# A float32 encoder trunk: the feed-forward input product turned round, with the input normalised before it is transposed

## The chip, the core and the metric

The kernel runs on one core of a Trainium2 chip. The metric is device time in microseconds (us) of one execution, from profiled and unprofiled runs of the same program; lower is better. TensorE is the matrix engine (PE in the profile, its weight loads PEld), VectorE is DVE, ScalarE is ACT, GpSimd is POOL, and SP is the engine that issues most DMA transfers.

## What is computed

256 tokens of width 1024 pass through four layers. Each layer has a feed-forward block, a token mixer (HGRN2, differential attention, pooling, then HGRN2 again) and a second feed-forward block: twelve sub-layers, eight of them feed-forward. Every sub-layer is normalised before and after, all in float32.

```python
def rmsnorm(x, w):
    y = xf * lax.rsqrt(jnp.mean(xf * xf, axis=-1, keepdims=True) + NORM_EPS)
    return (y * w)

def swiglu(x, w_in, w_out):          # w_in 1024 x 5632, w_out 2816 x 1024
    g, u = jnp.split(x @ w_in, 2, axis=-1)
    return (jax.nn.silu(g) * u) @ w_out

h = h + 0.5 * rmsnorm(swiglu(rmsnorm(h, gn[0]), ffn1_w_in[i], ffn1_w_out[i]), gn[1])
h = h + rmsnorm(mixer(rmsnorm(h, gn[2])), gn[3])
h = h + 0.5 * rmsnorm(swiglu(rmsnorm(h, gn[4]), ffn2_w_in[i], ffn2_w_out[i]), gn[5])
```

## The kernel before

**A float32 product in three.** Every float32 operand of a large product is kept as two float32r parts, high and low (`wh`, `wl` for weights, `xTh`, `xTl` for the transposed input, a pair of `hT` tiles for the hidden values). A product is the sum of three float32r products: high by high, high by low, low by high (`passes`, L203).

**Tiles.** The tokens lie in two tiles of 128. The residual stream is `h[0]`, `h[1]` (128 tokens x 1024). `pre` (L265) transposes the raw `h` of a token tile, eight 128x128 blocks on PE (L238), and splits the result into `xTh`, `xTl` (L274, L275). The norm before a sub-layer is not applied there: its gain is multiplied into the weights when these are split (L174 on ACT, L175 on DVE, each in pieces of 128x512), and its factor per token, 1/rms, is applied to the product at its end (`factors`, L278; `self.rs[t]` in `glu`).

**Weights.** All weights are used once per run and stream from DRAM in units of 1 MB (`fetch`, L148, issued by SP). `pump` splits a unit into two pairs `wh`, `wl`: units that carry a gain by L174 and L175, the others in pieces of 128x1024 by L169 on ACT and L170 on DVE.

**The feed-forward block** (`ffn`, L371) goes through eleven chunks of 256 hidden columns. For chunk c and token tile t there are these steps:

- `p` (`project`, L210, products on L207): the normalised input times 512 columns (256 of the gate half, 256 of the other half). The stationary operand is a 128x128 block of `xT`, the moving one 512 columns of weights; eight blocks of the inner dimension times three gives 24 products into one PSUM bank `s1` (shown as `s`), with tokens on the partitions. `glu` (L361) makes sigmoid (ACT, L366) and two multiplications (DVE, L367, L368) of it: `hh`, 128 tokens x 256.
- `t` (`split_T`, L241): two transposes of `hh` on PE (L238), then the split into the parts `hT` on ACT and DVE (L247, L248).
- `s` (`emit_out`, L219, products on L231): `hT` as the stationary operand times 1024 columns of the second weights into `acc[t]`, 12 products.

The steps are written out by hand in a string; from chunk 2 on, one chunk is

```python
todo += f" p{c}0 p{c}1 t{c}0"
todo += f" s{c - 1}0 s{c - 1}1 t{c}1" if c < e - 1 else f" t{c}1"
```

The last chunk (e = 10) is done by token tile, so that the residual of tile 0 runs beside the products of tile 1.

**Between sub-layers.** `residual` (L284) squares `acc` in two halves (ACT, L293), multiplies by the gain (DVE, L294, tile `tt`), makes the factor on POOL in three operations (L259, L261, L262) and adds into `h` in four pieces (DVE, L299). `turn` then calls `pre` for that token tile behind the next block of products. So the transposes of tile 0 stand behind the last input product of tile 1, and those of tile 1 behind the first block of the next sub-layer. This happens at eleven boundaries, twice each.

**Who sets the order.** The program is written as a list of operations; a scheduler places each on its engine's queue by priority and by its own estimate of when operands are there, and each engine then works through its queue in order. Code under `high_priority` is placed early; the splitting of weights is placed late (by LAG).

Of the kernel before, what the change touches and what calls it, by code (L numbers as in the profile page):

```python
# [9 lines left out]
F32 = mybir.dt.float32  # L10
# [30 lines left out]
# columns of the constant array  # L41
# [43 lines left out]
def grouped(w, cols):  # L85
    """[.., 1024, n] -> [.., chunk, half, 128, 4 k-tiles, 512]; cols lists each chunk's column runs."""
# [28 lines left out]
class Trunk:  # L115
    def __init__(self, ctx, tc, a, out, plan):
# [16 lines left out]
        self.units, self.loaded, self.ready, self.live, self.place = [], [], [], {"in": 0, "out": 0}, None  # L133
# [3 lines left out]
    def room(self, kind):  # L137
        """an FFN's second weights live in that FFN's own pool; kind is "in" or that FFN's place"""
# [4 lines left out]
    def fetch(self, parts=1):  # L143
        src, kind, gain = self.units.pop(0)
# [4 lines left out]
        self.loaded.append((r, kind, gain))  # L149

    def pump(self):
        nc = self.nc
        while True:
# [4 lines left out]
            if self.loaded and self.room(self.loaded[0][1]):  # L158
                r, kind, gain = self.loaded.pop(0)
# [4 lines left out]
                for j in range(2):  # L164
# [3 lines left out]
                    if gain is None:  # L168
                        nc.scalar.copy(wh, x)  # L169
                        nc.vector.tensor_sub(wl, x, wh.bitcast(F32))  # L170
                    else:
                        for k in range(2):
                            s, g = slice(k * 512, k * 512 + 512), self.gains[:, gain + 2 * j + k:gain + 2 * j + k + 1]
                            nc.scalar.activation(wh[:, s], x[:, s], AF.Copy, scale=g)  # L174
                            nc.vector.scalar_tensor_tensor(wl[:, s], x[:, s], g, wh[:, s].bitcast(F32),  # L175
                                                           op0=ALU.mult, op1=ALU.subtract)
# [20 lines left out]
    def in_units(self, w, i, j, n):  # L197
        """n chunks of an input product, gained by norm_gains[i, j]"""
        g = (i * 3 + j // 2) * KD
# [685 lines left out]
```

## Time and profile before

| | |
|---|---|
| device time, median of 3 runs | 2004.21 us (2003.1 to 2005.03) |
| the profiled execution, first to last instruction (span) | 2004.7 us |
| PE busy | 1977.9 us, 99% of the span |
| weight loads on PE (beside the products) | 1630.4 us, 81% |
| DVE busy | 1325.6 us, 66% |
| ACT busy | 1177.7 us, 59% |
| POOL busy | 81.7 us, 4% |
| granted PE clock, mean | 0.999 |
| moved by DMA | 358.56 MB, 179 GB/s |

The profiled execution is 0.5 us above the median of the runs. The page lists busy time by engine, the clock in 40 slices, the chain of work that ended last, and the costliest groups of instructions by line. A group's mean duration on PE is that of one product alone; products overlap, so the distance from one product's start to the next one's is what a stream of them costs.

### The profile page before, as it was taken

The page shows a single profiled execution, that of the slowest core. Times are in us where ns is not written, and L with a number is a line of the kernel's source. Part 1 is how long each engine was busy: PE and PEld are TensorE (multiplying, and loading weights), DVE is VectorE, ACT ScalarE, POOL GpSimd, SP SyncE. Part 2 cuts the span into 40 slices and gives each one's busy share as a digit, 9 for nine tenths or more (in the row PEclk, how much of TensorE's full clock was granted, in tenths as well). Part 3 has the DMA queues.
Part 4 walks back from the last instruction along what each step waited for, and adds up shares of the span by engine and source line. Part 5 has one row for each costly group of instructions (what it writes and reads, how often), then busy time and mean ns, then how long its engine had stood idle before and what let it go on. Part 6 is the DMA issues. An engine that isn't in the chain of part 4 may idle for free.

```text
span 2004.7 us, 25370 instructions
## 1 busy us (share of the span) xinstructions
PE 1977.9 (99%) x9320; PEld 1630.4 (81%) x9320; DVE 1325.6 (66%) x2356; ACT 1177.7 (59%) x2080; POOL 81.7 (4%) x189
## 2 busy tenths in 40 slices
PE   8999999999999999999999999999999999999998
PEld 6888888888888887788888888788888888888886
DVE  7765666866576658776667655676576657768652
ACT  7655786755565556665556545555465557767541
POOL 0000001000000000100000000000000000010000
PEclk9999999999999999999999999999999999999999
DMA  7753342755365534375536554465555534426540
GB/s 275 267 188 123 149 168 85 263 213 186 141 232 187 188 123 155 114 265 210 187 139 232 188 189 146 144 252 198 180 180 209 188 127 162 177 85 253 217 149 22
DMA packets 55003, 358.56 MB, mean 179 GB/s; under 512 B 7008, under 2 KB 10080, under 8 KB 13024
## 3 DMA queue, kind: packets, MB, share of 16 engines
q1 hardware_dynamic: 54016, 356.31, 49.4%
q8 instruction: 74, 1.21, 0.2%
q10 hardware_dynamic: 864, 0.64, 0.1%
q14 instruction: 49, 0.40, 0.1%
HBM read 355.86 MB, written 1.06 MB: 178 GB/s over the span
## 4 chain that ended last, share of the span: by engine, by line
PE 88%; issue 5%; DVE 3%; ACT 2%; POOL 1%; DMA 1%; POOLq 0%; DVEq 0%; SPq 0%; ACTq 0%
PE s L207 54%; PE acc L231 24%; PE tr L238 3%; PE acc L207 3%; DVE wl L175 1%; PE acc L633 1%; PE acc L577 1%; POOL ro L262 1%; ACT wh L174 0%; PE acc L817 0%; DMA h<-in_x_dram 0%; ACT junk L293 0%; DVE wl L170 0%; PE acc L627 0%; DMA lbraw<-in_hgrn_lb_raw_dram 0%
## 5 line engine op out<-in xcount | busy, mean ns | idle before, releaser
L207 PE MATMUL s<-wh,xTh 128*128 128x512 f32 x1792 | 712.0, 397 | 3.4 <-ACT wh L174 3.4
L207 PE MATMUL s<-wh,xTl 128*128 128x512 f32 x1792 | 701.0, 391 | 0.0
L207 PE MATMUL s<-wl,xTh 128*128 128x512 f32 x1792 | 699.9, 391 | 0.3 <-DVE wl L175 0.3
L175 DVE SCALAR_TENSOR_TENSOR wl<-raw,gains,wh 128x512 fp32r<-128x512 f32 x896 | 622.3, 745 | 66.3 <-ACT wh L174 66.0
L174 ACT ACTIVATE wh<-raw,gains 128x512 fp32r<-128x512 f32 x896 | 594.1, 720 | 92.3 <-PE s L207 58.8
L231 PE MATMUL acc<-wh,hT 128*128 128x512 f32 x1472 | 426.0, 397 | 0.6 <-ACT en L581 0.6
L207 PEld LDWEIGHTS s<-wh,xTl 128*128 128x128 f32 x1792 | 337.1, 188 | 71.5
L207 PEld LDWEIGHTS s<-wh,xTh 128*128 128x128 f32 x1792 | 337.3, 188 | 70.5 <-ACT wh L174 4.2
L207 PEld LDWEIGHTS s<-wl,xTh 128*128 128x128 f32 x1792 | 337.8, 188 | 67.1 <-DVE wl L175 1.1
L170 DVE TENSOR_TENSOR wl<-raw,wh 128x1024 fp32r<-128x1024 f32 x208 | 251.2, 1222 | 162.3 <-ACT wh L169 157.3
L169 ACT CAST wh<-raw 128x1024 fp32r<-128x1024 f32 x208 | 215.1, 1051 | 175.8 <-DMA raw<-in_ffn_w_out_dram 89.6
L231 PEld LDWEIGHTS acc<-wh,hT 128*128 128x128 f32 x1472 | 267.7, 188 | 51.5 <-ACT en L581 1.0
L366 ACT ACTIVATE sig<-s,ro 128x256 f32<-128x256 f32 x176 | 83.3, 473 | 278.0 <-PE s L207 277.5
L367 DVE SCALAR_TENSOR_TENSOR sig<-s,ro,sig 128x256 f32<-128x256 f32 x176 | 84.5, 480 | 219.6 <-ACT sig L366 219.5
L231 PE MATMUL acc<-wl,hT 128*128 128x512 f32 x736 | 228.5, 391 | 0.0
L231 PEld LDWEIGHTS acc<-wl,hT 128*128 128x128 f32 x736 | 138.1, 188 | 29.7
L247 ACT CAST hT<-tr 128x256 fp32r<-128x256 f32 x200 | 73.3, 367 | 80.1 <-PE tr L238 80.1
L248 DVE TENSOR_TENSOR hT<-tr,hT 128x256 fp32r<-128x256 f32 x200 | 83.2, 416 | 43.1 <-ACT hT L247 43.1
L368 DVE SCALAR_TENSOR_TENSOR hh<-s,ro,sig 128x256 f32<-128x256 f32 x176 | 84.1, 478 | 2.6
L294 DVE TENSOR_TENSOR tt<-acc,gpost 128x512 f32<-128x512 f32 x48 | 33.0, 688 | 66.5 <-ACT junk L293 66.5
L293 ACT ACTIVATE junk<-acc 128x512 bf16<-128x512 f32 x48 | 28.4, 592 | 75.0 <-PE acc L207 67.8
L238 PEld LDWEIGHTS tr<-ident,hh 128*128 128x128 f32 x352 | 48.4, 140 | 25.1 <-issue 2.3
(133 smaller groups left out, 1158.7 us busy)
## 6 DMA issues: line engine op xcount, KB each, us to landing
raw<-in_ffn_w_in_dram SPq DMA_DIRECT2D x174, 1024.0 KB, 4.8
raw<-in_ffn_w_out_dram SPq DMA_DIRECT2D x88, 1024.0 KB, 4.8
raw<-in_hgrn_w_in_dram SPq DMA_DIRECT2D x32, 1024.0 KB, 4.9
raw<-in_diff_w_in_dram SPq DMA_DIRECT2D x12, 1024.0 KB, 4.9
raw<-in_hgrn_w_out_dram SPq DMA_DIRECT2D x8, 1024.0 KB, 5.0
gpost<-in_post_gains_dram SPq DMA_DIRECT2D x12, 512.0 KB, 4.5
raw<-in_diff_w_out_dram SPq DMA_DIRECT2D x4, 1024.0 KB, 4.8
raw<-in_pool_w_in_dram SPq DMA_DIRECT2D x4, 1024.0 KB, 4.7
```

The lines of the kernel that those rows point to most:

```text
L169: nc.scalar.copy(wh, x)
L170: nc.vector.tensor_sub(wl, x, wh.bitcast(F32))
L174: nc.scalar.activation(wh[:, s], x[:, s], AF.Copy, scale=g)
L175: nc.vector.scalar_tensor_tensor(wl[:, s], x[:, s], g, wh[:, s].bitcast(F32), op0=ALU.mult, op1=ALU.subtract)
L207: self.nc.tensor.matmul(out, lhsT=x[:, lc], rhs=y[:, rc], start=start and i == 0, stop=stop and i == 2)
L231: self.nc.tensor.matmul(acc[:, s], lhsT=hT[a][:, j * P:(j + 1) * P], rhs=unit[j][b][:, s], start=first and j + a + b == 0, stop=False)
L238: self.nc.tensor.transpose(ps[:, j * P:(j + 1) * P], s, self.ident)
L247: nc.scalar.copy(hh, ps[:, :256])
L248: nc.vector.tensor_sub(hl, ps[:, :256], hh.bitcast(F32))
L366: nc.scalar.activation(sig, ps[:, :FC], AF.Sigmoid, scale=r)
L367: nc.vector.scalar_tensor_tensor(sig, ps[:, :FC], r, sig, op0=ALU.mult, op1=ALU.mult)
L368: nc.vector.scalar_tensor_tensor(hh, ps[:, FC:], r, sig, op0=ALU.mult, op1=ALU.mult)
```

## The change

The change rewrites the middle chunks of the feed-forward block (2 to 9 of eleven; 64 chunks in the run), and the norm before every sub-layer.

- In a middle chunk the steps `p` and `t` give way to two steps `P`. `project_T` makes the stationary operand of a 128x128 block of the weights, and the moving one of both token tiles' `xT`, 2 x 128 columns. The result has hidden columns on the partitions and 256 tokens along the free dimension, which is the layout `emit_out` wants. So there are 96 products of 256 columns in place of 48 of 512, and no transposes. `glu` works on that layout, and `split` makes the parts from `hh` in SBUF.
- For the moving operand to span both token tiles, `xTh` and `xTl` are now one tile each with both token tiles in it.
- A factor per token can no longer be applied per partition at the end of such a product. So `pre` now normalises first: the factor is made from `h` (two squares on ACT, two operations on POOL, in `token_factor`), `h` is multiplied by factor and gain on DVE (tile `tt`), and that is transposed. All sub-layers use it. The gain comes as a 512 KB broadcast per sub-layer (`next_gain`).
- The gain leaves the weights: every unit is split in pieces of 128x1024.
- `residual` makes its factor the same way, with both squares ahead of the multiplications and two POOL operations in place of three.

```diff
         self.wp = pool("wp", PIECES)
-        self.xp = pool("xp", 2)
-        self.hp = pool("hp", 16)
         self.gp = pool("gp", 1)
+        self.gq = pool("gq", 1)
...
                     x = r[:, j * 1024:(j + 1) * 1024]
-                    if gain is None:
-                        nc.scalar.copy(wh, x)
-                        nc.vector.tensor_sub(wl, x, wh.bitcast(F32))
-                    else:
-                        for k in range(2):
...
+                    nc.scalar.copy(wh, x)
+                    nc.vector.tensor_sub(wl, x, wh.bitcast(F32))
...
+    def project_T(self, j, units):
+        ps = self.s1p.tile([P, 2 * SEQ], F32, name="s1")
+        pieces = [p for u in units for p in u]
+        for half in range(2):
+            out = ps[:, half * SEQ:(half + 1) * SEQ].rearrange("p (t s) -> p t s", t=NT)
+            for k in range(KD):
+                col = (k % 2) * 512 + half * FC + j * P
+                wh, wl = (w[:, col:col + P] for w in pieces[k // 2])
+                xh, xl = (x[:, :, k * P:(k + 1) * P] for x in self.xT)
+                for n, (w, x) in enumerate(((wh, xh), (wh, xl), (wl, xh))):
+                    self.nc.tensor.matmul(out, lhsT=w, rhs=x, start=k + n == 0, stop=k == KD - 1 and n == 2)
+        return ps
...
+    def token_factor(self, src, post):
+        nc, sm = self.nc, self.sm
+        junk = self.nm.tile([P, 512], BF16, name="junk")
+        ss, x, o = (sm.tile([P, n], F32, name=f"tf{n}{i}") for i, n in enumerate((2, 1, 1)))
+        for n in range(2):
+            a = slice(n * 512, n * 512 + 512)
+            nc.scalar.activation(junk, src[:, a], AF.Square, scale=1.0 / (post * math.sqrt(D)),
+                                 accum_out=ss[:, n:n + 1])
+        nc.gpsimd.tensor_scalar(x, ss[:, 0:1], ss[:, 1:2], EPS / (post * post), op0=ALU.add, op1=ALU.add)
+        nc.gpsimd.tensor_tensor(o, x, self.power[:, :1], op=ALU.pow)
+        return o
+    def next_gain(self):
+        self.gpre = self.gq.tile([P, D], F32, name="gpre")
+        i, j = self.gain_rows.pop(0)
+        self.nc.sync.dma_start(self.gpre, self.a["pre_gains"][i, j // 2].partition_broadcast(P))
     def pre(self, t):
         nc = self.nc
-        xh = self.xp.tile([P, D], F32R, name="xTh")
-        xl = self.xp.tile([P, D], F32R, name="xTl")
+        with self.tc.high_priority():
+            r = self.token_factor(self.h[t], 1.0)
+            x = self.nm.tile([P, D], F32, name="tt")
+            for n in range(2):
+                s = slice(n * 512, (n + 1) * 512)
+                nc.vector.scalar_tensor_tensor(x[:, s], self.h[t][:, s], r, self.gpre[:, s],
+                                               op0=ALU.mult, op1=ALU.mult)
+        xh, xl = (y[:, t] for y in self.xT)
...
-            ps = self.transposed([self.h[t][:, n * 512 + j * P:n * 512 + (j + 1) * P] for j in range(4)])
+            ps = self.transposed([x[:, n * 512 + j * P:n * 512 + (j + 1) * P] for j in range(4)])
...
+        if t == NT - 1 and self.gain_rows:
+            self.next_gain()
...
+    def split(self, src):
+        nc = self.nc
+        hh = self.mx.tile([P, 256], F32R, name="hT", bufs=self.parts)
+        hl = self.mx.tile([P, 256], F32R, name="hT", bufs=self.parts)
+        nc.scalar.copy(hh, src)
+        nc.vector.tensor_sub(hl, src, hh.bitcast(F32))
+        return self.halves(hh, hl)
...
+        def both(c, jj):
+            ps = self.project_T(jj, weights(c))
+            used(("in", c), "in")
+            for t, parts in enumerate(self.split(self.glu(ps))):
+                hT[c, t, jj] = parts
...
         for c in range(2, e):
-            todo += f" p{c}0 p{c}1 t{c}0"
-            todo += f" s{c - 1}0 s{c - 1}1 t{c}1" if c < e - 1 else f" t{c}1"
+            todo += f" P{c}0 P{c}1"
+            if c < e - 1:
+                todo += f" s{c - 1}0 s{c - 1}1"
```

What the scheduler made of it is shown at three places. The first is PE in a middle chunk of the first feed-forward block. Before, at the end of chunk 2's input product (`s1` is the PSUM tile of an input product, `acc` of an output product, `tr` of transposes):

```order
L207 MATMUL s1_542<-wh_360,xTl_188 128x512
L238 MATMUL tr_610<-ident_88,hh_538 128x128 x2
L231 MATMUL acc_479<-wh_368,hT_400 128x512 x2
L231 MATMUL acc_479<-wl_369,hT_400 128x512 x2
...
L231 MATMUL acc_499<-wh_372,hT_496 128x512 x2
L238 MATMUL tr_641<-ident_88,hh_606 128x128 x2
L207 MATMUL s1_648<-wh_378,xTh_106 128x512
```

And now, at the same place:

```order
L222 MATMUL s1_539<-xTh_85,wl_344 128x256
L237 MATMUL acc_448<-wh_349,hT_377 128x512 x2
L237 MATMUL acc_448<-wl_350,hT_377 128x512 x2
...
L237 MATMUL acc_468<-wh_353,hT_464 128x512 x2
L222 MATMUL s1_651<-xTh_85,wh_359 128x256
L222 MATMUL s1_651<-xTl_86,wh_359 128x256
L222 MATMUL s1_651<-xTh_85,wl_360 128x256
```

The transposes on either side of the 24 output products are gone; 48 products of 256 columns stand in each of the two `P` steps. The three products of a block use `wh` twice in a row and then `wl`.

The second place is PE at the start of the sub-layer behind the first feed-forward block, where token tile 1 is transposed. Before:

```order
L207 MATMUL s1_1821<-wh_1535,xTl_1724 128x512
L238 MATMUL tr_1859<-ident_88,h1_103 128x128 x4
L238 MATMUL tr_1866<-ident_88,h1_103 128x128 x4
L207 MATMUL s1_1880<-wh_1543,xTh_1723 128x512
L207 MATMUL s1_1880<-wl_1544,xTh_1723 128x512
```

Now:

```order
L198 MATMUL s1_2117<-wh_1802,xTl_86 128x512
L198 MATMUL s1_2117<-wh_1930,xTh_85 128x512
L244 MATMUL tr_2101<-ident_87,tt_2098 128x128 x4
L198 MATMUL s1_2117<-wl_1931,xTh_85 128x512
L244 MATMUL tr_2108<-ident_87,tt_2098 128x128 x4
L198 MATMUL s1_2117<-wh_1930,xTl_86 128x512
```

The transposes stood behind the 24 products of that sub-layer's first block (`s1_1821`). They now stand inside its second block (`s1_2117`), behind 13 of its 24 products, so 35 products after the last output product of tile 1 (two of the first block stand ahead of that one). Those of tile 0 moved in the same way, to behind nine products of the step after the 24 of the last input product.

The third place is DVE at the same boundary, for token tile 0, now:

```order
L316 TENSOR_TENSOR tt_1898<-acc_448,gpost_222 128x512 x2
L320 SCALAR_TENSOR_TENSOR h0_91<-tt_1898,tf12_1893,h0_91 128x256 x4
L168 TENSOR_TENSOR wl_1931<-raw_1679,wh_1930 128x1024
L168 TENSOR_TENSOR wl_1935<-raw_1679,wh_1934 128x1024
L296 SCALAR_TENSOR_TENSOR tt_1963<-h0_91,tf12_1958,gpre_197 128x512 x2
L383 TENSOR_TENSOR sig_1950<-s1_1905,sig_1950 128x256
```

Between the residual (L320) and the new multiplication by factor and gain (L296) two splits of weights stand, in the time in which ACT and POOL make the factor.

## Rows read from the trace of the kernel before

**Rows 1.** The page: busy time by engine, and the granted clock in 40 slices.
```profile
PE 1977.9 (99%) x9320; PEld 1630.4 (81%) x9320; DVE 1325.6 (66%) x2356; ACT 1177.7 (59%) x2080; POOL 81.7 (4%) x189
PEclk9999999999999999999999999999999999999999
```
**Rows 2.** The chain of waits in a middle chunk: start us, us, what.
```profile
79.19 10.92 PE s L207 x48
90.11 0.22 PE tr L238 x2
90.33 5.48 PE acc L231 x24
...
96.03 10.92 PE s L207 x48
```
**Rows 3.** Groups by line: shapes, count | busy us, mean ns | idle before, releasers.
```profile
L207 PE MATMUL s<-wh,xTh 128*128 128x512 f32 x1792 | 712.0, 397 | 3.4 <-ACT wh L174 3.4
L207 PE MATMUL s<-wh,xTl 128*128 128x512 f32 x1792 | 701.0, 391 | 0.0
...
L175 DVE SCALAR_TENSOR_TENSOR wl<-raw,gains,wh 128x512 fp32r<-128x512 f32 x896 | 622.3, 745 | 66.3 <-ACT wh L174 66.0
...
L170 DVE TENSOR_TENSOR wl<-raw,wh 128x1024 fp32r<-128x1024 f32 x208 | 251.2, 1222 | 162.3 <-ACT wh L169 157.3 <-issue 0.3
...
L238 PE MATMUL tr<-ident,hh 128*128 128x128 f32 x352 | 67.2, 272 | 0.6 <-DVE hh L368 0.6
...
L238 PE MATMUL tr<-ident,h 128*128 128x128 f32 x192 | 28.8, 288 | 7.1 <-DMA ident<-in_consts_dram 4.0 <-DVE h L299 2.2 <-DMA h<-in_x_dram 0.8
```
**Rows 4.** Timeline of PE's weight loads, HGRN2's sums: start us, us, engine, line, operation.
```profile
215.28 0.19 PEld L577 LDWEIGHTS acc<-tri,ll 128*128 128x128 f32 x1
215.39 0.19 PEld L578 LDWEIGHTS acc<-tri,ll 128*128 128x128 f32 x1
215.62 0.19 PEld L577 LDWEIGHTS acc<-tri,lh 128*128 128x128 f32 x1
...
216.30 0.19 PEld L207 LDWEIGHTS s<-wh,xTh 128*128 128x128 f32 x1
```
**Rows 5.** Timeline of PE in the pooling mixer, first and last of a run of 16.
```profile
1250.48 0.39 PE L802 MATMUL tr<-band,u 128*128 128x128 f32 x2
...
1252.27 0.39 PE L817 MATMUL acc<-pT,wg 128*128 128x128 f32 x2
```
**Rows 6.** Products of two lines: duration ns min/median/max, first and last start.
```profile
L578 PE MATMUL acc<-tri,lh x32: 220/222/227, 215.3 to 1778.8; 128*128 128x128 f32 x32
...
L802 PE MATMUL tr<-band,u x32: 272/275/275, 1235.6 to 1258.8; 128*128 128x128 f32 x32
```
**Rows 7.** Timeline at a boundary, tile 1: ACT's first square, POOL's last operation, DVE's sum.
```profile
203.51 0.60 ACT L293 ACTIVATE junk<-acc 128x512 bf16<-128x512 f32 x1 [3.80 <-PE acc L207]
...
206.28 0.55 POOL L262 TENSOR_TENSOR ro<-rx,power 128x1 f32<-128x1 f32 x1
...
206.87 1.67 DVE L299 SCALAR_TENSOR_TENSOR h<-tt,ro,h 128x256 f32<-128x256 f32 x4 [0.50 <-POOL ro L262]
```
**Rows 8.** The chain of waits at the start.
```profile
3.96 8.87 DMA h<-in_x_dram
...
15.33 5.60 PE s L207 x17
```
**Rows 9.** Timeline of PE at the start: two products.
```profile
16.41 0.63 PE L207 MATMUL s<-wl,xTh 128*128 128x512 f32 x1
16.84 0.63 PE L207 MATMUL s<-wh,xTl 128*128 128x512 f32 x1
```
**Rows 10.** Busy time by engine in the first 20 us and in one chunk; clock, DMA share, GB/s.
```profile
0.00:20.00 20.00, 12.29 (x37) 9.23 (x38) 10.31 (x15) 12.61 (x20) 1.90 (x9) 1.00 0.80 286
79.19:96.03 16.84, 16.84 (x77) 13.87 (x77) 10.19 (x17) 9.89 (x16) 0.00 (x0) 1.00 0.72 265
```
**Rows 11.** Transfers by line: count, KB each, median us to landing.
```profile
gpost<-in_post_gains_dram SPq DMA_DIRECT2D x12, 512.0 KB, 4.5
```

More of the change, by code (lines that the diff above doesn't have):

```diff
@@ L148, in fetch @@
             self.nc.sync.dma_start(r[:, s], src[:, s])
-        self.loaded.append((r, kind, gain))
+        self.loaded.append((r, kind))
     def pump(self):
@@ L195, in free, with in_units @@
         self.pump()
-    def in_units(self, w, i, j, n):
-        g = (i * 3 + j // 2) * KD
-        return [[(w[c, 0], "in", g), (w[c, 1], "in", g + 4)] for c in range(n)]
+    def in_units(self, w, n):
+        return [[(w[c, 0], "in"), (w[c, 1], "in")] for c in range(n)]
     def passes(self, out, left, lc, right, rc, start, stop):
@@ L307, in turn @@
         while self.turns:
-            t = self.turns.pop(0)
-            self.pre(t)
-            self.factors(t)
+            self.pre(self.turns.pop(0))
     def run(self):
@@ L379, in used, with weights @@
                 self.free(1 if kind == "out" else 2, kind)
-        def first(c, t):
+        def weights(c):
             if c not in win:
@@ L385, in first, with turned @@
                     wout[c - 1], = self.take(1)
-            ps = self.project(t, win[c])
+            return win[c]
+        def first(c, t):
+            ps = self.project(t, weights(c))
             used(("in", c), "in")
-            g = self.glu(t, ps)
+            g[c, t] = self.glu(ps)
             self.turn()
-            return g
+        def turned(c, t):
+            for jj, parts in enumerate(self.split_T(g.pop((c, t)))):
+                hT[c, t, jj] = parts
[3 more added lines that the diff above has]
+            for t, parts in enumerate(self.split(self.glu(ps))):
+                hT[c, t, jj] = parts
         def second(c, t, js=range(2)):
@@ L396, in second @@
                 wout[c], = self.take(1)
-            self.emit_out(acc[t], hT[c, t], wout[c], c == 0, c == NFC - 1, js)
+            self.emit_out(acc[t], [hT.get((c, t, jj)) for jj in range(2)], wout[c], c == 0, c == NFC - 1, js)
             if 1 in js:
@@ L411, in ffn @@
             if what == "p":
-                g[c, t] = first(c, t)
+                first(c, t)
+            elif what == "P":
+                both(c, t)
             elif what == "t":
-                hT[c, t] = self.split_T(g.pop((c, t)))
+                turned(c, t)
             elif what in "sab":
@@ L418, in ffn @@
                 self.close(t, acc[t])
-        self.place = None
+        self.place, self.parts = None, 14
     def later(self, key, stage, lag=1):
@@ L471, in hgrn_units @@
         a, b = self.a["hgrn_w_in"][i // 3], self.a["hgrn_w_out"][i // 3]
-        u = sum(self.in_units(a, i, j, 2 * HP), [])
-        return u + [(b[p], "in", None) for p in range(4)]
+        u = sum(self.in_units(a, 2 * HP), [])
+        return u + [(b[p], "in") for p in range(4)]
     def lower_bound(self):
@@ L672, in diff_units @@
         a, b = self.a["diff_w_in"][i // 3], self.a["diff_w_out"][i // 3]
-        u = sum(self.in_units(a, i, j, 2 + HP), [])
-        return u + [(b[p], "in", None) for p in range(4)]
+        u = sum(self.in_units(a, 2 + HP), [])
+        return u + [(b[p], "in") for p in range(4)]
     def diff(self, i, j):
@@ L784, in pool_units @@
         a, b = self.a["pool_w_in"][i // 3], self.a["pool_w_out"][i // 3]
-        u = sum(self.in_units(a, i, j, 2), [])
-        return u + [(b[p], "in", None) for p in range(4)]
+        u = sum(self.in_units(a, 2), [])
+        return u + [(b[p], "in") for p in range(4)]
     def pool(self, i, j):
@@ L811, in group @@
             for gl in range(2):
-                hh = self.hp.tile([P, 256], F32R, name="hT")
-                hl = self.hp.tile([P, 256], F32R, name="hT")
+                hh = self.mx.tile([P, 256], F32R, name="hT", bufs=self.parts)
+                hl = self.mx.tile([P, 256], F32R, name="hT", bufs=self.parts)
                 for e in range(2):
```

108 lines of the change are left out of this document (43 added, 65 removed).

## Prediction, on record before the changed kernel ran

> **What bounds the kernel now.** I read the page first. PE is busy 99% of the span and its clock stands at 9 in all 40 slices [rows 1]; a busy PE need not be a full one, so the next view is the chain of waits. In a middle chunk the chain never leaves PE [rows 2]: 48 input products in 10.92 us, two transposes in 0.22, 24 output products in 5.48, two more transposes in 0.22, and the next chunk begins 16.84 us after the last. The pitch of a 512-column product is 10.92 / 48 = 0.2275 us, whatever its group's mean duration says (391 or 397 ns, [rows 3]): the products overlap. The groups show that input products waited for weights only 3.4 us in the run, the transposes of `hh` 0.6 us for their source, and those of `h` 7.1 us, 4.8 of it for the first transfers [rows 3]. DVE and ACT, at 10.19 and 9.89 us of a 16.84 us chunk, and DMA, at 0.72, have room [rows 10]. So the time is the sum of what stands in PE's queue, plus the start and the end. A change pays by what it takes out of that queue or puts into it.
>
> **The change, part by part.**
>
> *Taken out of PE's queue.* Four transposes in each of 64 chunks: 4 x 0.11 us [rows 2] = 0.44 us, times 64 = 28.2 us.
>
> *Put in: the price of a 256-column product.* 64 x 48 = 3072 products of 512 columns become 6144 of 256, each with its own load of 128 stationary columns, so 3072 loads are added. The trace has no product of 256 float32r columns; I bound it by neighbours.
> - Below: the shortest distance from load to load. Where products of 512 and 128 columns alternate, a pair takes 215.62 - 215.28 = 0.34 us, of which the short one has 0.1125 [rows 4]. The pooling mixer's float32 products of 128 columns come 16 in 1.79 us, 0.112 each [rows 5]. No product with a load of its own is cheaper, so a 256-column one costs at least 0.112.
> - Above: a straight line through 128 columns (0.1125) and 512 columns (0.2275) gives 0.151 at 256.
> - Half of 512 columns: 0.1138, if all of the 0.2275 grows with the columns.
> - Half with a surplus that stays: at 2.4 GHz 512 columns last 0.2133 us, so each product carries 0.0142 us more. If that comes once per product and load, 256 columns cost 0.1067 + 0.0142 = 0.1208.
>
> I take 0.1138. The nearest row is that of the float32 products [rows 5]: they load 128 columns too, and they stream as long as 256 float32r columns would. Float32r durations grow from 222 ns at 128 columns to 391 at 512 [rows 3, 6], 0.44 ns a column; the float32 product of 128 columns lasts 275 [rows 6], 53 ns or 120 columns more than the float32r one, so it counts as some 248. Load and stream are of equal length there and the pitch is still 0.112, with 0.005 on top of 0.1067, not 0.014. So I read most of the surplus as growing with float32r columns. Then 96 x 0.1138 = 10.92 us, just what 48 products cost before: this edit is worth zero, between -11 us (0.112) and +229 (0.151), with +43 at 0.1208.
>
> By the Trainium skill's page "TensorE: Matmul & The Clock Gate", section "Back-to-back issue gap", an isolated product costs N / 2.4 ns and a fixed 2.5 ns. With 2.5 ns of the 227.5 fixed, 256 columns would cost 0.1150 and the edit +7 us, an estimate from that page; the row of the float32 products does not contradict it.
>
> *Added: the norm ahead of the transposes.* PE's queue holds as many transposes of the input as before; what changes is when their source is there. At the first boundary the residual of tile 1 ran from its first square at 203.51 to 206.87 + 1.67 = 208.54, 5.0 us [rows 7]. The new residual is 0.4 us shorter (one POOL operation fewer, squares not held up by DVE). Then comes a second factor. The first one took 206.87 - 203.51 = 3.36 us [rows 7]; here one square runs beside the last half of the sum, and POOL has one operation fewer, so about 2.3. Then two multiplications at 0.745, the price of DVE's same operation on 512 columns [rows 3]. Sources ready: 4.6 + 2.3 + 0.75 = 7.65 us and 8.4 us after the last output product. PE gets there 33 products later for tile 0, 7.5 us, and 35 later for tile 1, 8.0 us, the second half at 8.2 and 8.6. So the products cover the chain to within a few tenths. At the two HGRN boundaries the tile `tt` also takes a mask from DRAM first, and DVE a sigmoid's product, perhaps 1.5 us each. I put 22 turns at 6 us together: nothing at best; if each chain slips by one weight split of 1.22 us [rows 3], 27 more.
>
> *Weights.* One split of 1222 ns replaces two of 745 [rows 3]: DVE and ACT gain time that PE does not wait for. Worth nothing; if the coarser pieces came late at a chunk's start, PE would wait up to 0.5 us, and only where the pool of split weights has run dry, which 3.4 us of waits in the run speak against.
>
> *`glu` and `split` on the new layout.* Same operations; the parts are wanted a chunk later, 16 us, and the two PSUM banks of input products are freed 5.5 us ahead of need. Nothing.
>
> *The gain's transfers.* 12 x 512 KB, like `gpost`'s, which take 4.5 us [rows 11], 1.8% more bytes at a DMA share of 0.72. In SP's queue the next gain waits until `pre(1)` has read the last one, some 8 us behind the last product, with weight transfers queued behind it; before, `gpost` held them up in the same place until about 5. That is 3 us of lead at 11 boundaries, against split weights for two and a half chunks in store. Nothing; 30 us if the store were empty each time.
>
> *The start.* The first transposes now need the gain, which is queued behind the last piece of `h`, landed at 12.83 [rows 8]. 0.5 MB at 286 GB/s [rows 10] is 1.8 us more: 14.7. Multiplication, transposes and copy take about 2: the first product at 16.8. It then needs 24 products for the first block, which ended at 15.33 + 5.60 = 20.93 [rows 8]. PE's pitch up to there was 16.84 - 16.41 = 0.43 us [rows 9], the level of 1.2 GHz after a stretch of waits (the granted clock of these rows reads 1.00 and does not show it). At that pitch the block ends at 27.0, at 0.2275 at 22.3: 1.4 to 6.1 later. I take +4.
>
> *The end.* The last residual is 0.4 us shorter.
>
> **Sum.** -28.2 + 0 + 6 + 4 - 0.4 = -18.6, from the profiled 2004.7 to 1986.1. The shown median is 0.5 below its profile, so 1985.6.
>
> **The rivals.**
>
> 1. *The surplus is paid per load* (slower). Two operands of 4 bytes a column are read at once, load and stream; in a 512-column product the load overlaps half of the stream, in a 256-column one all of it. Then 0.1208: +43 - 18.6, 2028 us. For it: the 0.0142 us in every 512-column pitch, which the trace does not explain. Against: the float32 pitch of 0.112. It decides from 18.6 / 6144 = 0.0030 above 0.1138, at 0.1168.
> 2. *The short product is worse than either* (0.151; strided reads over two token tiles could do it). +229 - 18.6: 2214 us. Against: nothing in the rows at 128 columns hints at it.
> 3. *Load and stream in turn.* 0.1125 + 0.1138 = 0.226: +690 - 18.6, 2676 us. Against: 512 columns would then take 0.33, and take 0.2275. The skill's same page, section "The mechanism", has loads overlap running products only when the row groups differ, which would be this case; by the rows the trace disagrees.
> 4. *The norm becomes the wait.* 2 us at each of 22 turns instead of 0.27: +38 - 18.6, 2024 us. It decides from 0.85 us more a turn, less than one weight split on DVE. For it: DVE and ACT work in order, and two splits stand between sum and multiplication. Against: 35 products of cover, and before only 2.2 us of waits for `h` in the run.
> 5. *It comes to nothing:* a pitch between 0.1162 and 0.1174, or half of rival 4. Within 4 us of before.
>
> **How the numbers follow.** My forecast, a pitch of 0.112 to 0.116 with turns covered, 0.55, by itself 1970 to 1998. Rival 1, 0.22; rival 2, 0.05; rival 3, 0.01; rival 4, 0.08; rival 5, 0.09. 0.2% of the time is 4 us, about what a measurement of this kernel can tell from no change. Faster 0.55, same 0.09, slower 0.36. The range goes from 1970 (0.112, turns free) to 2031, beyond rivals 1 and 4; left out are rivals 2 and 3 and the tails, some 0.15.
>
> **What would show it.** In the chain, the 96 products of two `P` steps lasting 10.9 us with 24 output products behind them and no transposes, chunks 16.4 us apart; 11.6 would be rival 1. In the groups, idle time ahead of the transposes of `tt` of a few us in all, not tens. At the start, the first block ending at 22 to 27. I am wrong if the pitch is above 0.117, or if PE waits for `tt` over 20 us.

## The result, and the profile after

The changed kernel takes **2033.4 us** (median of 4 runs, 2032.8 to 2035.9); the kernel before, beside it, 2004.6 (2003.1 to 2006.9). The ratio is 1.0144, 95% interval 1.0129 to 1.0158: slower by 29 us, where I had forecast 18.6 us faster, and just past the range's end. The profiled execution took 2032.8 us, its span 2031.1.

The page of the changed kernel, busy time by engine and the granted clock:

```profile
PE 1990.0 (98%) x12136; PEld 1754.7 (86%) x12136; DVE 1248.2 (61%) x1954; ACT 1043.6 (51%) x1682; POOL 78.8 (4%) x165
PEclk9999999999999999999999999999999999999999
```

As in [rows 1], PE is the bound, and its granted clock stands at 9 in all 40 slices (mean 0.999). PE has 2816 products and transposes more, DVE and ACT fewer instructions than before. The chain of waits in the middle chunks (start us, us, what):

```profile
65.58 11.36 PE s L222 x96
76.94 5.45 PE acc L237 x24
82.39 11.36 PE s L222 x96
```

The transposes are gone from the chain, 0.44 us a chunk, as the change says. But the 96 products take 11.36 us where 48 took 10.92 [rows 2]: 0.1183 us each, not 0.1138. That is 0.44 us too, so a chunk still takes 82.39 - 65.58 = 16.81 us, against 16.84. What the change takes out, its products put back.

The groups by line (shapes, count | busy, mean ns | idle before):

```profile
L222 PE MATMUL s<-xTh,wh 128*128 128x256 f32 x2048 | 575.4, 281 | 0.0
...
L198 PE MATMUL s<-wh,xTh 128*128 128x512 f32 x768 | 308.9, 402 | 0.0
...
L198 PE MATMUL s<-wh,xTl 128*128 128x512 f32 x768 | 304.4, 396 | 0.0
```

L198 is the old 512-column input product (L207 before), of which 2304 are left in the mixers and in the first and last chunks. The change does nothing to it, and yet its mean is 402 and 396 ns where [rows 3] have 397 and 391. A mean is the duration of one product and not the distance to the next, so here is the timeline of PE in an HGRN2 block, the first two and the last of 11 products:

```profile
228.09 0.40 PE L198 MATMUL s<-wl,xTh 128*128 128x512 f32 x1
228.32 0.39 PE L198 MATMUL s<-wh,xTl 128*128 128x512 f32 x1
...
230.42 0.40 PE L198 MATMUL s<-wh,xTl 128*128 128x512 f32 x1
```

Ten steps in 2.33 us: a pitch of 0.233, against 0.2275. The third part is at the boundaries. PE's waits:

```profile
PE tr L244 <- DVE tt L296: 27.2, 19, 15.6
```

15.6 of it is the start, 11.6 lie at the boundaries, where the transposes of `h` had waited 2.2 [rows 3], so 9.4 were added. And the start's own chain:

```profile
5.70 8.97 DMA gpre<-in_pre_gains_dram
...
15.57 1.97 PE tr L244 x8
...
21.58 8.64 PE s L198 x37
```

The gain landed at 14.67. The first block's 24th product is the 17th of the last row, so the block ended at 21.58 + 17 x 8.64 / 37 = 25.6, 4.6 us after the 20.93 of [rows 8]. Where chunk 2 begins, the lag is 48.61 - 45.39 = 3.2 us, partly since the kernel before waits for split weights in between (0.47 us in the first line; the other two are the first product of chunk 2, before and after):

```profile
23.43 0.51 PE L207 MATMUL s<-wh,xTh 128*128 128x512 f32 x1 [0.47 <-ACT wh L174]
...
45.39 0.40 PE L207 MATMUL s<-wh,xTh 128*128 128x512 f32 x1
```
```profile
48.61 0.28 PE L222 MATMUL s<-xTh,wh 128*128 128x256 f32 x1
```

So the 26.4 us between the two spans come from: middle chunks 64 x (16.81 - 16.84) = -2; 512-column products 2304 x 0.0055 = +13; waits at the boundaries +9.4; the start some +3. Together that is +23, and some 3 us are not assigned. The experiments take these apart.

### The profile page after: what moved, and what is told of

It is laid out like the page before. It is cut to its first block, busy times and chain, and to the rows that moved or that the text cites. A ratio compares the mean times of both kernels' runs of the same rounds, so it can differ in the third digit from the quotient of the medians.

```text
span 2031.1 us, 30076 instructions
## 1 busy us (share of the span) xinstructions
PE 1990.0 (98%) x12136; PEld 1754.7 (86%) x12136; DVE 1248.2 (61%) x1954; ACT 1043.6 (51%) x1682; POOL 78.8 (4%) x165
## 4 chain that ended last, share of the span: by engine, by line
issue 57%; PE 35%; ACT 2%; POOL 2%; DVE 2%; DMA 1%; SPq 0%; POOLq 0%; DVEq 0%; ACTq 0%
PE s L198 14%; PE s L222 9%; PE acc L237 7%; PE acc L198 2%; PE tr L244 1%; PE acc L673 1%; POOL tf L279 1%; PE acc L617 1%; ACT wh L167 1%; POOL tf L278 1%; ACT junk L276 0%; DMA raw<-in_ffn_w_in_dram 0%; DMA gpre<-in_pre_gains_dram 0%; DVE tt L296 0%; PE acc L667 0%
## 5 line engine op out<-in xcount | busy, mean ns | idle before, releaser
L168 DVE TENSOR_TENSOR wl<-raw,wh 128x1024 fp32r<-128x1024 f32 x656 | 782.9, 1221 | 357.8 <-ACT wh L167 353.1
L167 ACT CAST wh<-raw 128x1024 fp32r<-128x1024 f32 x656 | 663.9, 1048 | 308.4 <-DMA raw<-in_ffn_w_out_dram 143.2
L222 PE MATMUL s<-xTh,wh 128*128 128x256 f32 x2048 | 575.4, 281 | 0.0
L222 PE MATMUL s<-xTh,wl 128*128 128x256 f32 x2048 | 575.3, 281 | 0.0
L222 PE MATMUL s<-xTl,wh 128*128 128x256 f32 x2048 | 575.1, 281 | 0.0
L222 PEld LDWEIGHTS s<-xTl,wh 128*128 128x128 f32 x2048 | 386.2, 189 | 2.8
L222 PEld LDWEIGHTS s<-xTh,wl 128*128 128x128 f32 x2048 | 385.8, 188 | 0.0
L198 PE MATMUL s<-wh,xTh 128*128 128x512 f32 x768 | 308.9, 402 | 0.0
L198 PE MATMUL s<-wl,xTh 128*128 128x512 f32 x768 | 304.4, 396 | 0.0
L198 PE MATMUL s<-wh,xTl 128*128 128x512 f32 x768 | 304.4, 396 | 0.0
L198 PEld LDWEIGHTS s<-wh,xTl 128*128 128x128 f32 x768 | 144.3, 188 | 34.5 <-DVE xTl L304 0.2
L198 PEld LDWEIGHTS s<-wh,xTh 128*128 128x128 f32 x768 | 144.4, 188 | 32.4 <-ACT xTh L303 0.2
L198 PEld LDWEIGHTS s<-wl,xTh 128*128 128x128 f32 x768 | 144.5, 188 | 31.6
```

Of the source, the lines that this page charges most:

```text
L198: self.nc.tensor.matmul(out, lhsT=x[:, lc], rhs=y[:, rc], start=start and i == 0, stop=stop and i == 2)
L222: self.nc.tensor.matmul(out, lhsT=w, rhs=x, start=k + n == 0, stop=k == KD - 1 and n == 2)
```

## The experiments

The title of an experiment, or the bracket behind it, names the kernel that it edits; "kernel of 1" is that of experiment 1. Behind "Measured" stand the median device time, its ratio to the kernel before, which ran beside it, and the 95% interval of that ratio.

All slow products touch xT, and the output products do not, so the first theories are about where the operands lie. In the built programs, xTh and xTl began at bytes 132384 and 140576 of each partition before, 32 above a multiple of 64, like all split weights. In the changed kernel they are the first tiles of the pool `fix`, at 16512 and 24704, both multiples of 64; the weights are still 32 above one. "Offset" below means this place modulo 64.

**1. xT moved by 32 bytes** (changed kernel)
```
+        self.power = self.fix.tile([P, 2], F32, name="power")
...
         self.h, self.xT = [], [self.fix.tile(...) for n in "hl"]
...
         self.ident = self.fix.tile([P, P], F32, name="ident")
...
-        self.power = self.fix.tile([P, 2], F32, name="power")
```


> The changed kernel, with the tile `power` (32 bytes a partition) allocated ahead of the two xT tiles instead of behind them: xT moves up by 32 bytes, from a multiple of 64 to 32 above one, where all the split weights already lie; nothing else moves. Offset theory (a float32r product is slow where the addresses of its two operands differ by 32 bytes modulo 64): the 96 products of two P steps last 10.9 us instead of 11.36 (0.1138 a product instead of 0.1183), the 512-column input products go back from 0.234 to 0.227, and the time falls by 6144 x 0.0045 + 2225 x 0.007 = 43 us, to 1990. Place theory (xT lies low in SBUF, or both token tiles share one tile): nothing changes, 2033. Load theory (rival 1: 256 columns pay a surplus with each load): 0.1183 stays; at most the 512-column products recover, 2018.

Measured: 2037.0 us, 1.0152 (1.0135 to 1.0169). In the chain of waits:
```profile
66.08 11.52 PE s L222 x96
77.59 5.47 PE acc L237 x24
83.07 11.52 PE s L222 x96
```
The 512-column products did go back: the L198 groups' means fell to 399 and 392 to 393, and the median distance from one to the next to 0.227. But the 256-column ones got slower, 11.52 / 96 = 0.1200. The offset theory is right for the one and wrong for the other. And 0.1200 is what rival 1 had said (0.1208): the 0.0133 us by which a 512-column product exceeds 512 columns at 2.4 GHz are paid in full by one of 256 (0.1067 + 0.0133).

**2. The kernel before, xT moved onto a multiple of 64**
```
+        self.sp = [pool(f"sp{n}") for n in range(1)]
         self.xp = pool("xp", 2)
+        self.sp.append(pool("sp1"))
...
+        for sp in self.sp:
+            nc.gpsimd.memset(sp.tile([P, 2], F32, name="spare"), 0.0)
```


> The kernel before, with 32 spare bytes ahead of the xT tiles and 32 behind them: xT moves to a multiple of 64, the weights stay 32 above one; no product changes. Offset theory: all 5376 input products go from 0.227 to about 0.234, the time to 2004.6 + 5376 x 0.0065 = 2040, with the output products still at 0.227. Place theory: 2004.6, as before, since xT stays high in SBUF and in tiles of its own. Load theory: 2004.6.

Measured: 2032.6 us, 1.0133 (1.0118 to 1.0148). The chain:
```profile
61.41 11.19 PE s L209 x48
...
72.83 5.48 PE acc L233 x24
```
11.19 / 48 = 0.2331 for the input products, with the output products where they were [rows 2]. No product was changed, and the tiles behind xT moved by 64 bytes and so kept their offset. That moving xT by 32 bytes costs 27 us of 2005 is shown; why an address does this is not. In the changed kernel the same offset costs 2304 products about 0.0056 us each, 13 us by this estimate.

**3. Weights moved instead, everything on multiples of 64** (changed kernel)
```
         nc.gpsimd.memset(self.power, -0.5)
+        self.spare = self.fix.tile([P, 2], F32, name="spare")
+        nc.gpsimd.memset(self.spare, 0.0)
```


> The changed kernel, with 32 spare bytes behind the tiles of the fix pool: xT stays on a multiple of 64, and all the split weights move onto multiples of 64 too. Offset theory (the difference of the two operands decides): both fast again, 0.1138 and 0.227, 1990 us. Absolute theory (an operand on a multiple of 64 is slow in itself): input products stay at 0.117 and 0.234 and the output products, whose weights now lie on multiples of 64, join them, 2033 + 2200 x 0.0065 = 2047. Place and load theory: 2033.

Measured: 2025.2 us, 1.0095 (1.008 to 1.011).
```profile
64.87 11.31 PE s L222 x96
76.18 5.46 PE acc L237 x24
```
0.1178 for 256 columns. The 512-column input products stand between, at distances of 0.226, 0.229 and 0.232 by turns, and the output products stay at 0.227, which excludes the absolute theory. The offset theory (the difference of the two operands decides) fails too: with both operands on multiples of 64 the 512-column products are slower than with both 32 above one. No theory here explains that 256-column products are fastest where the 512-column ones are not; what else of the addresses matters stays open. All offsets tried left them between 0.1178 and 0.1200, well above 0.1138.

**4. No P steps: the norm's part alone** (kernel of 1)
```
-            todo += f" P{c}0 P{c}1"
-            if c < e - 1:
-                todo += f" s{c - 1}0 s{c - 1}1"
+            todo += f" p{c}0 p{c}1 t{c}0"
+            todo += f" s{c - 1}0 s{c - 1}1 t{c}1" if c < e - 1 else f" t{c}1"
```


> The first experiment's kernel (xT moved by 32 bytes) with the middle chunks put back as they were: p, p, t, s, s, t steps with 512-column products and transposes of hh, and the norm still ahead of the transposes. So it holds only the norm's part of the change. If the P step saves its four transposes a chunk and 256 columns cost half of 512, this one is 28 us slower than the first experiment's. If the norm's part costs what the trace of the changed kernel suggests (12 us at the waits for tt, 3 at the start), it takes 2004.6 + 12 to 15 = 2017 to 2020. If 256-column products pay a surplus with each load the distance to the first experiment is well below 28.

Measured: 2027.2 us, 1.0106 (1.009 to 1.0121). The norm's part (the norm ahead of the transposes, with the longer pieces of weights and the gain at the start) costs 21 us by itself. Against this kernel, experiment 1's P steps are not 28 us faster but 10 slower, as its chunks say: 83.07 - 66.08 = 16.99 against 16.83, times 64. PE's waits:
```profile
PE tr L244 <- DVE tt L296: 31.2, 23, 15.1
```
16.1 past the start in 22 turns. The timeline of one of them shows the chain (the last output product of tile 0 began at 531.50):
```profile
531.99 0.60 ACT L276 ACTIVATE junk<-acc 128x512 bf16<-128x512 f32 x1 [3.75 <-PE acc L198]
...
533.88 0.56 POOL L279 TENSOR_TENSOR tf<-tf,power 128x1 f32<-128x1 f32 x1
...
534.63 1.67 DVE L320 SCALAR_TENSOR_TENSOR h<-tt,tf,h 128x256 f32<-128x256 f32 x4
...
535.62 0.63 ACT L276 ACTIVATE junk<-h 128x512 bf16<-128x512 f32 x1
...
536.25 1.04 ACT L167 CAST wh<-raw 128x1024 fp32r<-128x1024 f32 x1
...
537.19 0.62 ACT L276 ACTIVATE junk<-h 128x512 bf16<-128x512 f32 x1
...
538.01 0.73 POOL L278 TENSOR_SCALAR tf<-tf 128x1 f32<-128x1 f32 x1 [3.57 <-ACT junk L276]
...
538.82 0.56 POOL L279 TENSOR_TENSOR tf<-tf,power 128x1 f32<-128x1 f32 x1
...
539.41 1.42 DVE L296 SCALAR_TENSOR_TENSOR tt<-h,tf,gpre 128x512 f32<-128x512 f32 x2 [0.84 <-POOL tf L279]
540.31 0.63 PE L244 MATMUL tr<-ident,tt 128*128 128x128 f32 x4 [0.93 <-DVE tt L296]
```
From the first square to the first transpose 8.3 us pass, and 8.8 from the start of the last output product, for which the prediction had 7.65. The sum of the residual ends at 536.30; from there the second factor takes 3.1 us, not 2.3: its second square stands behind a copy of weights (536.25 to 537.29), and POOL's first operation takes 0.73. In the changed kernel it takes 3.1 us as well at the one turn read there, the first (196.17 to 199.29).

**5. wh loaded once for both parts of xT** (kernel of 1)
```
-                for n, (w, x) in enumerate(((wh, xh), (wh, xl), (wl, xh))):
-                    self.nc.tensor.matmul(out, lhsT=w, rhs=x, start=k + n == 0, stop=k == KD - 1 and n == 2)
+                x = self.xx[:, :, :, k * P:(k + 1) * P]
...
+                        self.nc.tensor.matmul(out, lhsT=wh, rhs=x, start=k == 0, stop=k == KD - 1)
...
+                        self.nc.tensor.matmul(out[:, 0], lhsT=wl, rhs=x[:, 0], start=False, stop=False)
+            s = self.mx.tile([P, 256], F32, name="hh", bufs=2)
+            self.nc.scalar.copy(s, ps[:, 256:])
+            self.nc.vector.tensor_add(s, ps[:, :256], s)
```


> The first experiment's kernel, with the P step's two products by wh made into one: the stationary 128 columns of wh meet xTh and xTl together, 512 columns into a PSUM bank, and wl meets xTh in 256 columns as before; ACT copies the bank's second half to SBUF and DVE adds the first (four pairs of these a chunk, some 1.6 us more for each engine in a chunk of 17). So 64 instead of 96 products a pair of P steps, with the same columns. Theory of a surplus with every product and its load (512 columns 0.2267, 256 columns 0.120): a triple takes 0.347 instead of 0.360, a pair of P steps 11.1 us instead of 11.5, 64 x 0.43 = 27 us less, 2010. Theory that reading xT as the moving operand is what costs (0.0133 with every 256 columns of it): 0.360 stays, 2037. If the PSUM banks or the engines' added work hold PE up, waits at L217's products show it.

Measured: 2018.8 us, 1.0073 (1.0055 to 1.0092); 18 us less than experiment 1. Two neighbouring groups of output products in the chain:
```profile
60.72 5.47 PE acc L245 x24
...
77.37 5.50 PE acc L245 x24
```
A chunk takes 16.65 us, not 16.99. Fewer products with the same columns are faster, so the surplus goes with the product and its load, and reading xT as the moving operand is not what costs. Which of the two brings it is not shown: every product here has a load of its own. Two thirds of the 27 us came: a triple took (16.65 - 5.48) / 32 = 0.349 rather than 0.347, and PE waited 3.0 us for the additions on DVE that free a PSUM bank.

**6. The kernel before, input products cut in two**
```
-            self.passes(ps, ..., slice((k % 2) * 512, (k % 2) * 512 + 512), ...)
+        for a in (0, 256):
+            for k in range(KD):
+                c = (k % 2) * 512 + a
+                self.passes(ps[:, a:a + 256], ..., slice(c, c + 256), ...)
```


> The kernel before, with each 512-column input product cut into two of 256, the stationary xT loaded for each; all 16 k-tiles' worth of one half come first, then the other. No P steps, no strided reads, operands where they were, so this is the price of the 256-column product by itself. Surplus with every product (0.120 against 0.2267 / 2): 5376 x 0.0133 = 71 us more, 2077. Half price, as my sum had it (0.1138): 2005. If the two-tile reads of xT in the P step were what made 0.120, also 2005.

Measured: 2070.5 us, 1.0329 (1.0313 to 1.0346): 66 us more. The chain:
```profile
64.31 11.50 PE s L207 x96
...
81.71 11.52 PE s L207 x96
```
0.1200 again, without P steps and without strided reads. This settles the price: with both operands 32 above a multiple of 64, 256 columns cost 0.1200 and 512 cost 0.227.

**7. The turns later in PE's order** (kernel of 4)
```
-        todo = "p00 p10 t00 p01 t10 p11 t01 s00 t11 s01"
+        todo = "p00 p10 n00 t00 s00 p01 t10 p11 t01 t11 s01"
...
-            todo += f" p{e}{t} s{e - 2}{t} a..."
+            todo += f" p{e}{t} s{e - 2}{t} n00 a..."
```
(`n` calls `turn()`, which `first` no longer does.)


> The fourth experiment's kernel (no P steps) with the turn, that is the next input's norm and transposes, placed later in PE's order: tile 0's behind the 12 output products that follow the last input block, tile 1's behind a second block of 24 input products, with tile 0's first output products moved ahead of tile 1's first input block to cover the copies of xT. If the norm's chain is simply longer than its cover (rival 4), the 16 us of waits for tt past the start go down to a few, and the time from 2027 to about 2011 to 2013. If the boundaries' cost lies elsewhere (in late weight splits, or in PE waiting for the copies of xT behind the transposes), it stays near 2027.

Measured: 2029.7 us, 1.0127 (1.0111 to 1.0143); no gain. The waits for `tt` past the start halved, from 16.1 to 7.8 us, but 4.2 us of waits for the copies of xT came in their place, and nothing was won in the whole.

**8. The edits of 5 and 7 together**

> The edits of the fifth and the seventh experiment together on the first's kernel: P steps with wh loaded once for xTh and xTl, and the turns later. If both theories hold: 2037 - 27 - 16 = 1994, faster than the kernel before by some 11 us. If only the price of the product was right, 2010; if only the turns, 2021.

Measured: 2022.1 us, 1.0086 (1.007 to 1.0102), 3 us more than experiment 5 alone, with runs that overlap (2018.9 to 2022.7 here, 2015.9 to 2022.6 there). More cover won nothing.

**9. Without the tokens' factor** (kernel of 4)
```
-            r = self.token_factor(self.h[t], 1.0)
...
-                nc.vector.scalar_tensor_tensor(x[:, s], self.h[t][:, s], r, self.gpre[:, s], ...)
+                nc.vector.tensor_mul(x[:, s], self.h[t][:, s], self.gpre[:, s])
```


> The fourth experiment's kernel (no P steps, xT by 32 bytes) without the tokens' factor ahead of the transposes: the tile tt is h times the gain alone, so the input's division by its root mean square is left out, and with it two squares on ACT, two operations on POOL and DVE's wait for them, some 2.3 to 3.5 us of the chain at each of 22 turns. Chain theory (the norm's steps, one behind the other, are longer than the products that cover them): the waits for tt past the start, 16 us, go to at most 3, and the time from 2027 to 2010 to 2013. Weights theory (the split weights in pieces twice as long stand in ACT's and DVE's queues ahead of the chain and delay whatever comes): most of it stays, 2020 or more.

Measured: 2017.7 us, 1.0068 (1.0053 to 1.0083). PE's waits:
```profile
PE tr L244 <- DVE tt L295: 16.5, 4, 14.8
PE tr L244 <- DVE hh L382: 3.9, 4, 1.3
```
The waits at the boundaries fell from 16.1 to 1.7, as the chain theory says, but the time by 9.4 only, between what the two theories expected; other waits, as that for `hh`, grew.

**10. The kernel before with the P steps of 5**, the tokens' factors repeated over the partitions through DRAM
```
...
+        nc.vector.tensor_mul(a, a, r)
+        nc.scalar.activation(sig, a, AF.Sigmoid)
+        nc.gpsimd.tensor_mul(b, b, r)
...
```


> The kernel before, with raw h transposed and the gain in the weights as it was, but with the P steps of the fifth experiment in the middle chunks (wh loaded once for xTh and xTl). The tokens' factors, which in the P step run along the free axis, go through DRAM to a tile that repeats them on all partitions, on POOL's queue, and gate and value are multiplied by it, one on DVE, one on POOL. So it has the P step's gain and none of the norm's cost. If costs add up as the runs so far have them (the fifth kernel against the fourth: 8.3 us less), 2004.5 - 8.3 = 1996, faster than both kernels. If the added work on DVE (some 3.4 us a chunk of 17) or the two PSUM banks hold PE up, 2005 or more, with waits at the first products of a half.

Measured: 2122.0 us, 1.0585 (1.0567 to 1.0604). ACT's waits, and ACT in a stretch of the timeline:
```profile
ACT wh L169 <- DMA raw<-in_ffn_w_out_dram: 96.7, 67, 6.3
ACT wh L174 <- DMA raw<-in_ffn_w_in_dram: 74.6, 22, 7.9
```
```profile
399.38 0.72 ACT L174 ACTIVATE wh<-raw,gains 128x512 fp32r<-128x512 f32 x1 [7.17 <-DMA raw<-in_ffn_w_in_dram]
400.01 0.46 ACT L394 ACTIVATE sig<-s,ro 128x256 f32<-128x256 f32 x1
```
ACT stood 7.17 us before a copy of weights that had not landed, with the sigmoid behind it that the next transposes of `hh` needed. PE waited 89.5 us for `hh` and `h` in the run. Its clock fell as well: behind this wait, in which PE stood from 397.4 to 402.1, the granted clock was 0.50 (1.2 GHz; the last column but two), and 0.986 on the mean of the run against 0.999:
```profile
402.10:404.80 2.70, 2.65 (x8) 2.20 (x9) 2.70 (x5) 2.42 (x4) 0.00 (x0) 0.50 0.64 267
```
The costs of single parts did not add up here: what the other engines' queues held came too late for PE, and the clock that fell with the waits added to it.

**11. Short splits of weights** (kernel of 4)
```
-                    nc.scalar.copy(wh, x)
-                    nc.vector.tensor_sub(wl, x, wh.bitcast(F32))
+                    for k in range(2):
+                        s = slice(k * 512, k * 512 + 512)
+                        nc.scalar.copy(wh[:, s], x[:, s])
+                        nc.vector.tensor_sub(wl[:, s], x[:, s], wh[:, s].bitcast(F32))
```


> The fourth experiment's kernel with the split of weights cut back to pieces of 512 columns, as they were before the change, without the gain: 656 more instructions each on ACT and DVE. Weights theory: pieces of 0.5 and 0.75 us stand in the chain's way for half as long, and half or more of the 16 us of waits for tt goes, 2019 or less. Chain theory: a few tenths at each turn at best, 2022 to 2027.

Measured: 2026.2 us, 1.0107 (1.009 to 1.0124), no difference clear of the spread of experiment 4 (2026.1 to 2028.1). At the turn shown there, the chain did become shorter:
```profile
533.29 0.60 ACT L278 ACTIVATE junk<-acc 128x512 bf16<-128x512 f32 x1 [3.75 <-PE acc L200]
...
537.62 0.61 ACT L169 CAST wh<-raw 128x512 fp32r<-128x512 f32 x1
...
541.15 0.63 PE L246 MATMUL tr<-ident,tt 128*128 128x128 f32 x4 [0.92 <-DVE tt L298]
```
The copy in the second square's way takes 0.61 instead of 1.04 us, and from the first square to the first transpose 7.9 us pass instead of 8.3. But the scheduler now placed the transposes behind 31 products instead of 33, so PE waited 0.92 us where it had waited 0.93. The same holds over all 22 turns: the mean fell from 8.5 to 7.9 us, and the waits stayed (17.0 past the start, 16.1 before). So the pieces do lengthen the chain, and this run does not show what they cost: the scheduler's estimate, which places the transposes, moved with them.

**12. The tenth kernel with the splits placed later**
```
-LAG = 100
+LAG = 160
...
-        nc.gpsimd.tensor_mul(b, b, r)
+        nc.vector.tensor_mul(b, b, r)
```


> The kernel of the tenth experiment with the split of weights put later in the engines' queues (LAG 160 instead of 100, since its chunks issue more instructions) and value's multiplication by the repeated factors on DVE instead of POOL. If the tenth was slow because ACT and DVE stood in order behind a split whose weights had not landed, with the sigmoids, PSUM copies and products that PE waits for behind it, those waits (ACT's 171 us for raw, PE's 110 us for hh and h) shrink and the time falls to between 1996 and 2010. If DVE has simply too much work in a chunk with these P steps, or the splits now come late for PE itself, it stays above 2060.

Measured: 2079.0 us, 1.0368 (1.035 to 1.0385). 43 us less by the two edits together, but still above the 2060 that was expected if DVE has too much work or the splits come late; ACT's waits for `raw` fell only from 171 to 142 us. Which of these holds it up is not shown. No version that was run beats the kernel before.

**13. Long splits alone, in the kernel before**
```
-        return [[(w[c, 0], "in", g), (w[c, 1], "in", g + 4)] for c in range(n)]
+        return [[(w[c, 0], "in", None), (w[c, 1], "in", None)] for c in range(n)]
```


> The kernel before with the input weights split as the changed kernel does it, in pieces of 1024 columns without the gain (the input norms' gains are left out); raw h is transposed as before and the tokens' factors follow the products. So only the longer pieces are added. Of the 21 us that the norm's part took, the kernel without the factor gave back 9. If the longer pieces on ACT and DVE cause the other 12, this one takes 2016. If it is the multiplication ahead of the transposes and the gain's transfers, 2005 or somewhat less, as my sum had it.

Measured: 2008.2 us, 1.002 (1.0011 to 1.003). The longer pieces cost 3.6 us in the kernel before, not 12, and not nothing either. Of the norm's 21 us, 9 are the factor's (experiment 9). The start's share is 1.7: chunk 2 begins at 47.12 in experiment 4's kernel and at 45.39 in the kernel before. The pieces' share lies between the 1 us of experiment 11, which is not clear of noise, and the 3.6 of this one, if costs add up. The rest, some 7 to 9 us, is not assigned to an edit. Read from the traces, most of the 21 is waits for `tt`: 16.1 us past the start, where the transposes of `h` had waited 2.2.

## Why the prediction was wrong, step by step

- **Transposes, -28.2.** Right: 0.44 us a chunk left the chain.
- **"I take 0.1138" for the 256-column product: the step that failed first.** It is 0.1183 where the change puts xT, above the 0.117 that the prediction gave as its sign of being wrong: 64 x 0.44 = +28 us instead of 0, and 0.1200 where the operands lie as before (experiments 1 and 6). Rival 1 had 0.1208, a chance of 0.22, and the surplus paid once with every product and its load, as the runs show it; that load and stream reading at once is the cause, as rival 1 says, no run shows. What led me off was the row I called nearest: the float32 products [rows 5] carry 0.005 us over their columns, and I moved that to float32r, while the float32r row at hand [rows 2] carried 0.0142. The likelier reading was to keep the surplus of the same kind of product. The Trainium skill's page "TensorE: Matmul & The Clock Gate", section "Back-to-back issue gap", gives an isolated product 2.5 ns over its columns; here the trace differs: 13.3 ns at 256 columns and 13.4 at 512, each with its own load. Rivals 2 and 3 (0.151 and 0.226) are out by the same rows.
- **The 512-column products, not in the sum at all.** I took their 0.2275 as fixed because no edit touches them. The new pool order moved xT by an odd multiple of 32 bytes against the weights, and each went to 0.233: +13 us, an estimate from 2304 products (experiment 2 shows the cause).
- **The norm's turns, +6.** 11.6 us of waits in the changed kernel, 9.4 more than before, and 14.8 with xT moved back (experiment 1), where the 512-column products run at 0.227 and so cover less. The chain was drawn right, each link in its place, but its second factor was 0.8 us longer than I put it at both turns that were read. This is rival 4, at 0.5 to 0.7 us a turn where it had 2. Experiment 9 shows the factor as the cause of the waits, and experiment 7 that a later place does not pay; experiment 11 leaves open what shorter pieces would give.
- **Weights splitting, 0.** 3.6 us in the kernel before (experiment 13). Small, but of the wrong sign for an edit that I expected to free DVE and ACT; DVE is indeed busy 77 us less.
- **The start, +4.** Near: the gain at 14.67 for 14.7, the first product at 17.5 for 16.8, the first block's end at 25.6 between 22.3 and 27; of that lag 3.2 us are left at chunk 2.
- `glu`, `split` and the gain's transfers: PE's longest waits hold nothing of them, as I said.

In sum: -28 (transposes) + 28 (256-column products) - 2 (output products, 5.45 us a chunk for 5.48) + 13 (512-column products) + 9 (turns) + 3 (start) = +23, against 26 between the spans and 29 between the medians; the rest is not assigned. Of the 45 us between the forecast span of 1986.1 and the measured 2031.1, 28 are the product's price and 13 the offset. One reading of the prediction was off as well: the 0.5 us by which it went from span to device time. In all runs here the device time is 1.7 to 2.4 us above the span of the same execution, so the 0.5, a span set against a median of device times, is no measure of that step; the forecast moves by some 2 us.

## What to carry to other kernels

A product that is cut in two pays its fixed part twice; take that part from the row of the same data type and load, not from one that merely streams as long, and ask for fewer, longer products first (experiment 5 won 18 us over experiment 1 that way). When pools are reordered, look at the operands' addresses: an unchanged line can become slower. And a chain of five small steps on three engines that must end within a fixed cover should be costed with one foreign instruction in each queue that it passes; where a scheduler decides how much cover there is, count the products between before you compare two waits (experiment 11).

## What was not expected of the hardware

- Moving one operand by 32 bytes against the other took float32r products of 512 columns from 0.227 to 0.233 us, and back (experiments 1 and 2).
- Products of 256 columns go the other way: 0.1200 without variation where both operands are 32 above a multiple of 64, 0.1178 where both are on one, 0.1183 with xT alone on one.
- Where a run of 512-column products begins after transposes, the first few stand 0.231 to 0.236 apart before 0.227 is reached, in the kernel before as in the others.
